# A two-layer encoder trunk on one core: layer 0's output banks emptied by ScalarE and gated on POOL, and a new layout of layer 1's last stage

## The chip, the cores and the metric

The kernel runs on one core of one Trainium2 chip. TensorE (PE) multiplies matrices, VectorE (DVE), ScalarE (ACT) and GpSimd (POOL) do the rest on rows of 128 partitions, and SyncE (SP) issues nearly all DMA transfers. The metric is the device time of one execution in microseconds. Each engine works through its own list of instructions in the order in which the program gives them, and waits at an instruction whose inputs or buffers aren't there yet.

## The reference, cut to what matters

2048 tokens of width 1024 go through two layers. Each layer modulates its input, mixes it, and adds the gated result to the residual ahead of a LayerNorm:

```python
h = x * (1.0 + scale) + shift                    # per layer, shift/scale/gate from c
y = even_mixer(h) if layer == 0 else odd_mixer(h)
x = layer_norm(DEEPNORM_ALPHA * x + gate * y, ln_g[layer], ln_b[layer])

# even_mixer: windowed attention and chunked spatial gating side by side, times silu(g), then
return y @ w_out                                 # (2048, 1024) @ (1024, 1024): the out-projection

# odd_mixer: in-projection, depthwise conv, two gated linear recurrences, then
y = rg_lru(forward) + rg_lru(reverse)            # h[s] = a[s] * h[s-1] + b[s], and the same from the end
return (y * silu(g)) @ w_out
```

The change touches the end of layer 0 (`gate * y` and the residual after the out-projection) and the end of layer 1 (the reverse recurrence's completion and its out-projection). Everything is float32.

## The kernel before, in words

**Matmuls.** The tokens are worked in four tiles `t` of 512. A float32 product is made of three matmuls (`mm3`, L158, L159, L160) on operands split in a high and a low half: the high half is a copy on ACT (L154), the low half a subtraction on DVE (L155). So each operand of a matmul costs one ACT and one DVE instruction, unless it was split earlier and parked in DRAM (`w_d`, `wo_d`).

**Layer 0's out-projection** (`project_out`) runs once per tile `t`. For each half `n` of the output columns, `job_tm` loads eight weight tiles (`raw`), splits each (`hl`) and accumulates into four PSUM banks, one for each 128 tokens. Six banks (`pja`, `px`, `pjb`, two each) go round, so that the next job takes over the banks of an earlier one. When the job is done, DVE multiplies each bank by the gate (`gz`, L753), which frees the bank, and adds ALPHA times the residual (`z`, L755). This makes 4 x 2 x 4 = 32 pairs of instructions. `sgate` is the stage ahead of it; its scratch tile `sq` (L693) stands in the same SBUF pool.

**Layer 1** sweeps forward over `t` = 0..3. Its forward recurrence is finished on the way; the reverse one needs the later tokens, so for t = 0..2 its inputs go to DRAM (`a_d`, `b_d`, `f_d`, `g_d`, `u_d`, `v_d`) and only t = 3 is finished at once: the reverse scan (L1007), the sum of both directions on POOL (L1017), the product with the gate (L1034), and the split into y3[0..7]. The out-projection of t = 3 (`part_out`) keeps its 8 banks over the whole end of the sweep, all PSUM that `pj` and `pm` have: k = 0..3 are added as soon as y3[0..3] are there, k = 4..7 at the end. The out weights wo[n][k] are loaded once and stay in SBUF for all four tiles (`resident`, L1079).

**The way back.** `load_y(t)` makes y for t = 2, 1, 0 from DRAM: for even k a reverse scan (L1113) from the carry of tile t+1, the carry to tile t and the sum with the forward part on POOL (L1116, L1117), and the gate product (L1118); for odd k one multiply-add with the carry (L1127) — both then split. Its tiles `at`, `bt`, `ft`, `gt`, `ut`, `vt` have two buffers each and are loaded on SP (L1106). Then come the out-projection of that tile, the residual rows (`z`, L1151; L1166 for t = 3, L1178 and L1195 for t = 2 and the rest) and the LayerNorm (`norm_rows`: L614, L616, L623, L624), with two POOL instructions for the reciprocal root (L150, L151).

**What sets the order.** The instructions are given in program order to a scheduler that simulates the engines and writes a fixed list for each; `high_priority` moves a piece ahead in it. Nothing is reordered on the chip. SBUF is a stack from each side: the left pool `oq` ("outq") opens where layer 1's front pool (`X`, `xc` and the like) has closed, the right pool `op` ("outp") where the recurrence's pool `rp` (`ra`, `T`, `ii`, `G`, `hg`) has closed. A tile that is laid over an old one waits until the old one's last reader is done, tile by tile.

Of the kernel before, what the change touches and what calls it, by code (L numbers as in the profile page):

```python
# [7 lines left out]
F32 = mybir.dt.float32  # L8
F32R = mybir.dt.float32r
I32 = mybir.dt.int32  # L10
AF = mybir.ActivationFunctionType
ALU = mybir.AluOpType
# [6 lines left out]
KD = D // 128  # L19
C = 512  # L20
NT = S // C
# [32 lines left out]
def kernel(  # L54
# [27 lines left out]
    nc = tc.nc  # L82
    act = nc.scalar.activation
    tt = nc.vector.tensor_tensor
# [154 lines left out]
    for i in range(2):  # L239
        nc.gpsimd.dma_start(out=vrow0[24 + 8 * i:32 + 8 * i].rearrange("k (a q) -> k a q", a=4),  # L240
                            in_=ada_b[1, i * D:i * D + D].rearrange("(a k q) -> k a q", a=4, q=32))
# [4 lines left out]
    ps = bank(px, "px")  # L246
# [22 lines left out]
    ps = bank(px, "px")  # L269
# [26 lines left out]
    ps = bank(px, "px")  # L296
# [331 lines left out]
    bp = pool(sd, "sgate", right)  # L628
    g_bc = bp.tile([128, D], F32, name="g_bc")
    b_bc = bp.tile([128, D], F32, name="b_bc")  # L630
    gate0 = bp.tile([128, D], F32, name="gate0")
# [6 lines left out]
    for g in range(2):  # L638
        wr = bp.tile([128, 4, 128], F32, tag="wsr", bufs=1, name="wsr")
        load(out=wr, in_=ev_sg_w[0, 4 * g:4 * g + 4].rearrange("g p q -> p g q"))  # L640
        ps = bank(pm, "pm")
# [6 lines left out]
    ps = bank(pm, "pm")  # L648
# [3 lines left out]
    for i in range(4):  # L652
        stt(out=bias_sg[:, i, :], in0=ps[:, i * 128:i * 128 + 128], scalar=vcol0[:, 52 + i:53 + i],
            in1=bias_sg[:, i, :], op0=ALU.mult, op1=ALU.add)
# [20 lines left out]
    def sgate(t, hT):  # L675
        cs = cols(w0, 1280)
        if t == 0:
            ps = sv_ps
            count[0] += KD
        else:  # L680
            ps = job_tm(lambda k: wunit(cs(k)), hT)
        sv = []
        for b in range(4):
            pv = ps[b].rearrange("p (g d) -> p g d", g=8)
            mu = bp.tile([128, 8], F32, tag="mu", bufs=2, name="mu")
            with tc.high_priority():
                nc.vector.tensor_reduce(out=mu, in_=pv, axis=AX.X, op=ALU.add)
                ts(out=mu, in0=mu, scalar1=-1.0 / 64.0, scalar2=None, op0=ALU.mult)
            v = bp.tile([128, 8, 64], F32, tag="sv", bufs=5, name="sv")
            sv.append(v)  # L690
            with tc.high_priority():
                tt(out=v, in0=pv, in1=mu[:, :, None].to_broadcast([128, 8, 64]), op=ALU.add)
            sq = bp.tile([128, 8, 64], F32, tag="sq", bufs=2, name="sq")  # L693
            act(out=sq, in_=v, func=AF.Square)
            var = bp.tile([128, 8], F32, tag="var", bufs=2, name="var")
            nc.vector.tensor_reduce(out=var, in_=sq, axis=AX.X, op=ALU.add)
            rsqrt_eps(var, var, 1.0 / 64.0)
            tt(out=v, in0=v, in1=var[:, :, None].to_broadcast([128, 8, 64]), op=ALU.mult)
# [4 lines left out]
        ps = job_cm(lambda k: ug0[k] if k < n0 else wunit(cg(k)), hT)  # L703
# [4 lines left out]
        ps = job_cm(lambda k: wunit(cu(k)), hT)  # L708
# [4 lines left out]
        for i in range(4):  # L713
            ps = bank(pm, "pm")
            for b in range(4):
# [5 lines left out]
                in1=bias_sg[:, i:i + 1, :].to_broadcast([128, 4, 128]), op0=ALU.mult, op1=ALU.add)  # L721
# [6 lines left out]
        ps = job_cm(lambda k: wunit(ca(k), perm=True), hT)  # L728
# [12 lines left out]
    def project_out(t, y):  # L741
        zt = []
        for b in range(4):
            z = bp.tile([128, D], F32, tag="z", bufs=5, name="z")
            load(out=z, in_=xs[t * C + b * 128:t * C + b * 128 + 128, :])
            zt.append(z)
        for n in range(2):
            cw = out_rows(w1, n * C)
            ps = job_tm(lambda k: wunit(cw(k)), y, (4, 5, 6, 7, 0, 1, 2, 3))
            for b in range(4):  # L750
                gz = bp.tile([128, C], F32, tag="gz", bufs=2, name="gz")
                with tc.high_priority():
                    tt(out=gz, in0=ps[b], in1=gate0[:, n * C:n * C + C], op=ALU.mult)  # L753
                zs = zt[b][:, n * C:n * C + C]
                stt(out=zs, in0=zs, scalar=ALPHA, in1=gz, op0=ALU.mult, op1=ALU.add)  # L755
        for b in range(4):
            r = t * C + b * 128
            norm_rows(bp, zt[b], x1_d[r:r + 128, :], g_bc, b_bc)
# [311 lines left out]
    def part_out(ps, hl, k):  # L1070
        for b in range(4):
            sl = slice(b * 128, b * 128 + 128)
            mm3(ps[b], y3[0][k][:, sl], y3[1][k][:, sl], hl[:, 0], hl[:, 1], k == 0, k == KD - 1)

    wo = [[None] * KD, [None] * KD]

    def resident(p, n, k):
        w = p.tile([128, 2, C], F32R, name=f"wo{n}_{k}")
        nc.sync.dma_start(out=w.bitcast(F32), in_=wo_d[n * KD + k])  # L1079
        wo[n][k] = w  # L1080
# [5 lines left out]
            part_out(ps3[n], wo[n][k], k)  # L1086

    oq = pool(ctx, "outq", left)
    for k in (4, 5):
        for n in range(2):  # L1090
            resident(oq, n, k)
    back(NT - 1, 1, f1, G1)
# [6 lines left out]
    def load_y(t):  # L1099
        y = ([], [])  # L1100
        n = C if t < NT - 2 else C - 2
        c0 = t * C

        def fetch(tag, src, k):
            p = oq.tile([128, C], F32, tag=tag, bufs=2, name=tag)
            load(out=p[:, 0:n], in_=src[:, k, c0:c0 + n])  # L1106
            return p

# [24 lines left out]
            y[1].append(lo[:, k % 2])  # L1133
        return y

    y2 = load_y(NT - 2)
    se.close()


    op = pool(ctx, "outp", right)  # L1140
    for k in (6, 7):
        for n in range(2):
            resident(op, n, k)
    for k in range(4, KD):
        for n in range(2):
            part_out(ps3[n], wo[n][k], k)

    def residual_tile(t, b):
        r = t * C + b * 128
# [4 lines left out]
    zt = [residual_tile(NT - 1, b) for b in range(4)]  # L1154
    g_bc = op.tile([128, D], F32, name="g_bc1")
    b_bc = op.tile([128, D], F32, name="b_bc1")
    load(out=g_bc, in_=ln_g[1:2, :].broadcast_to([128, D]))
    load(out=b_bc, in_=ln_b[1:2, :].broadcast_to([128, D]))
    def finish(t, b, z):
# [67 lines left out]
```

## Time and profile before

| | |
|---|---|
| runs of before | 1568.82, 1569.88, 1575.3 us; median 1569.88 us |
| the profiled execution | 1567.64 us, with a span of 1565.9 us from first to last instruction |
| mean granted TensorE clock in it | 0.983 |
| setup and attention, 0 to 440 us of the span | PE busy 410.3 of 440 us |
| layer 0's gating and out-projection, 440 to 905 | PE busy 451.4 of 465 us, DVE 351.1, ACT 160.3, POOL 68.3 |
| layer 1's sweep, 905 to 1395 | PE busy 473.7 of 490 us, DVE 384.4, ACT 351.5, POOL 196.2 |
| between y3[5] and y3[6], 1395 to 1413 | PE busy 0.2 of 18 us, DVE 15.4, ACT 4.9, POOL 8.2 |
| the way back, 1413 to 1566 | PE busy 144.7 of 153 us, DVE 120.0, ACT 11.4, POOL 41.9 |

A row of a timeline gives the start, the time taken, the engine, the line and the operation, then the tiles it writes and reads (buffer numbers left out), and in brackets how long the engine sat idle before it and what ended the idle time. "x2" is two instructions in one row. A row of the list of waits gives the sum, the number and the longest of such idle times. A row of windows gives, for a stretch of the span, its length, each engine's busy time, the granted clock (PEclk, 1.00 is full), the DMA engines' busy share and the GB/s moved. Two matmuls overlap in their pipeline, so in a full stream their starts lie closer together than their durations.

### The profile page before, as it was taken

What the parts mean: (1) busy time and instruction counts of PE and PEld (TensorE: products, weight loads), DVE (VectorE), ACT (ScalarE), POOL (GpSimd) and SP (SyncE); (2) the same over time, 40 slices, a digit from 0 to 9 for tenths busy, and PEclk for the clock granted to TensorE, in tenths of its full rate; (3) what the DMA queues carried; (4) which work ended last, traced back from release to release, by engine and by line L of the source; (5) the groups of instructions that cost most, each with busy time, mean ns of one, the idle gap of its engine ahead of it and who ended that gap; (6) DMA issues with size and microseconds to landing.
All of it is one profiled execution on the core that took longest, in us unless ns stands there. A gap on an engine that the chain in (4) does not pass through costs nothing. (4 is left out here: it accounts for less than half of the span.)

```text
span 1565.9 us, 22099 instructions
## 1 busy us (share of the span) xinstructions
PE 1480.2 (95%) x7096; PEld 1185.7 (76%) x7096; DVE 1186.2 (76%) x2180; ACT 784.1 (50%) x1470; POOL 404.7 (26%) x488
## 2 busy tenths in 40 slices
PE   7999999989999999999999999999999999869997
PEld 3887777657878777788887787787788788747886
DVE  4599889755859568967767775987987697788985
ACT  4677767542523332343244228499498496841100
POOL 1023233211005000300120231634644432133221
PEclk9999999999999999999999999999999999989999
DMA  9357766839788989988785699788777766369751
GB/s 348 130 170 219 224 196 189 265 120 304 243 281 298 257 255 298 314 276 262 260 296 177 195 263 275 231 259 283 224 249 271 236 226 220 111 204 340 257 193 54
DMA packets 209211, 370.91 MB, mean 237 GB/s; under 512 B 56616, under 2 KB 103620, under 8 KB 209096
## 3 DMA queue, kind: packets, MB, share of 16 engines
q1 hardware_dynamic: 202344, 354.53, 70.2%
q0 software_dynamic: 6752, 14.98, 3.7%
q8 instruction: 56, 0.92, 0.2%
q14 instruction: 59, 0.48, 0.1%
HBM read 261.96 MB, written 85.97 MB: 222 GB/s over the span
## 5 line engine op out<-in xcount | busy, mean ns | idle before, releaser
L154 ACT ACTIVATE hl<-raw 128x512 fp32r<-128x512 f32 x192 | 119.1, 628 | 227.3 <-DMA raw<-in_ev_w_in_dram 142.2
L159 PE MATMUL pj<-alo,hl 128*128 128x512 f32 x512 | 200.7, 392 | 0.0
L158 PE MATMUL pj<-ahi,hl 128*128 128x512 f32 x512 | 199.5, 392 | 1.1 <-DVE gz L753 1.1
L160 PE MATMUL pj<-ahi,hl 128*128 128x512 f32 x512 | 199.6, 391 | 0.0
L155 DVE TENSOR_TENSOR hl<-raw,hl 128x512 fp32r<-128x512 f32 x192 | 131.8, 695 | 71.5 <-ACT hl L154 70.7
L150 POOL TENSOR_SCALAR rstd<-mv 128x1 f32<-128x1 f32 x32 | 31.0, 970 | 416.5 <-DVE mv L616 305.8
L158 PEld LDWEIGHTS pj<-ahi,hl 128*128 128x128 f32 x512 | 96.5, 189 | 22.0 <-DVE gz L753 1.5
L159 PEld LDWEIGHTS pj<-alo,hl 128*128 128x128 f32 x512 | 96.6, 189 | 20.3
L160 PEld LDWEIGHTS pj<-ahi,hl 128*128 128x128 f32 x512 | 96.4, 188 | 20.2
L465 POOL DMA_DIRECT2D P<-T x112 | 62.6, 566 | 177.7 <-DVE nm L430 78.0
L158 PE MATMUL pj<-wqh,hhi 128*128 128x256 f32 (+1 forms) x256 | 88.5, 350 | 2.5 <-ACT hhi L154 1.7
L430 DVE CUSTOM_DVE_ANT_0 P<-psc,mask,nsink 128x384 f32<-128x384 f32 (+1 forms) x128 | 73.8, 593 | 22.1 <-PE psc L429 22.0
L154 ACT ACTIVATE phl<-praw 128x512 fp32r<-128x512 f32 x56 | 35.4, 631 | 105.9 <-DMA praw<-in_od_w_in_dram 51.1
L159 PE MATMUL pj<-wql,hhi 128*128 128x256 f32 (+1 forms) x256 | 88.0, 344 | 0.0
L160 PE MATMUL pj<-wqh,hlo 128*128 128x512 f32 (+1 forms) x256 | 85.7, 347 | 1.5 <-DVE hlo L155 1.5
L977 DVE SCALAR_TENSOR_TENSOR ii<-ii,xc 128x1024 f32<-128x1024 f32 (+2 forms) x32 | 40.6, 1269 | 57.6 <-ACT ii L971 57.6
L433 ACT ACTIVATE P<-P,nm 128x384 f32<-128x384 f32 (+1 forms) x128 | 76.4, 601 | 10.3 <-DVE nm L430 10.1
L777 POOL TENSOR_TENSOR alo<-hm,ahi 128x512 fp32r<-128x512 f32 x32 | 48.5, 1524 | 118.5 <-DVE hm L776 99.7
L947 DVE SCALAR_TENSOR_TENSOR xc<-X,vcol,xc 128x512 f32<-128x512 f32 (+2 forms) x96 | 75.2, 818 | 0.3
L158 PE MATMUL pm<-xhi,hg 128*128 128x512 f32 (+3 forms) x160 | 55.6, 361 | 14.1 <-ACT xhi L154 6.5
L155 DVE TENSOR_TENSOR phl<-praw,phl 128x512 fp32r<-128x512 f32 x56 | 39.1, 698 | 35.2 <-ACT phl L154 33.0
L775 ACT ACTIVATE ahi<-hm,shift,scale 128x512 fp32r<-128x512 f32 x32 | 25.2, 812 | 74.1 <-DVE hm L774 66.8
(304 smaller groups left out, 4320.1 us busy)
## 6 DMA issues: line engine op xcount, KB each, us to landing
hl<-w_d SPq DMA_DIRECT2D x128, 512.0 KB, 4.7
raw<-in_ev_w_in_dram SPq DMA_DIRECT2D x128, 256.0 KB, 4.0
w_d<-phl SPq DMA_DIRECT2D x40, 512.0 KB, 4.6
aw<-in_ada_w_dram SPq DMA_DIRECT2D x32, 512.0 KB, 6.9
hg<-w_d SPq DMA_DIRECT2D x32, 512.0 KB, 5.4
P<-T SPq DMA_DIRECT2D x104, 96.0 KB, 4.8
P<-T POOLq DMA_DIRECT2D x104, 96.0 KB, 4.2
aw<-in_ada_w_dram SPq DMA_DIRECT2D x8, 1024.0 KB, 7.7
```

What stands on the lines that cost most here:

```text
L150: nc.gpsimd.tensor_scalar(out=dst, in0=src, scalar1=mul, scalar2=EPS, op0=ALU.mult, op1=ALU.add)
L154: act(out=hi, in_=src, func=AF.Copy)
L155: tt(out=lo, in0=src, in1=hi.bitcast(F32), op=ALU.subtract)
L158: nc.tensor.matmul(ps, lhsT=ahi, rhs=bhi, start=first, stop=False)
L159: nc.tensor.matmul(ps, lhsT=ahi, rhs=blo, start=False, stop=False)
L160: nc.tensor.matmul(ps, lhsT=alo, rhs=bhi, start=False, stop=last)
L430: nc.vector.tensor_tensor_reduce(out=p[:, g, 0:W], in0=ps[:, 0:W], in1=mask[:, m0:m0 + W], scale=-0.125, scalar=nsink[:, h:h + 1], op0=ALU ...
L433: act(out=p[:, g, 0:W], in_=p[:, g, 0:W], func=AF.Exp, scale=-1.0, bias=nm[:, h:h + 1], accum_out=rs[:, h:h + 1])
L465: dma.dma_start(out=pv[32 * r:32 * r + 32, 0:nb, i], in_=T[32 * i:32 * i + 32, 0:nk].rearrange("p (j r) m -> p r j m", r=4)[:, r])
L777: nc.gpsimd.tensor_tensor(out=lo[:, j], in0=h, in1=hi[:, j].bitcast(F32), op=ALU.subtract)
L947: stt(out=xc[:, w], in0=xt[:, j0 + j:j0 + j + W], scalar=vcol1[:, 8 * j + g:8 * j + g + 1], in1=xc[:, w], op0=ALU.mult, op1=ALU.add)
L977: stt(out=ii[i][:, :, w], in0=ii[i][:, :, w], scalar=1.0, in1=xc[:, None, w].to_broadcast([128, 2, W]), op0=ALU.add, op1=ALU.mult)
```

## The change

In layer 0, ACT now copies each bank to `gz` and so frees it; POOL multiplies `gz` by the gate; the residual's addition stays on DVE. `gz` has three buffers in place of two, and `sq` one in place of two, in the same pool. At the end of layer 1, all eight out-weight tiles of k = 4..7 are in `oq` on the left (before, k = 6 and 7 were in `op` on the right, allocated after `load_y(2)`). The tiles of `load_y` move from `oq` to `op`, which opens only once the recurrence's pool has closed. In the program's text `load_y(2)` now comes after t = 3's residual rows and ahead of `part_out` for k = 4..7. Lines after L753 have a number one higher until the deleted lines of the end.

```diff
--- before.py
+++ after.py
@@ -690,7 +690,7 @@
             sv.append(v)
             with tc.high_priority():
                 tt(out=v, in0=pv, in1=mu[:, :, None].to_broadcast([128, 8, 64]), op=ALU.add)
-            sq = bp.tile([128, 8, 64], F32, tag="sq", bufs=2, name="sq")
+            sq = bp.tile([128, 8, 64], F32, tag="sq", bufs=1, name="sq")
             act(out=sq, in_=v, func=AF.Square)
             var = bp.tile([128, 8], F32, tag="var", bufs=2, name="var")
             nc.vector.tensor_reduce(out=var, in_=sq, axis=AX.X, op=ALU.add)
@@ -748,9 +748,10 @@
             cw = out_rows(w1, n * C)
             ps = job_tm(lambda k: wunit(cw(k)), y, (4, 5, 6, 7, 0, 1, 2, 3))
             for b in range(4):
-                gz = bp.tile([128, C], F32, tag="gz", bufs=2, name="gz")
+                gz = bp.tile([128, C], F32, tag="gz", bufs=3, name="gz")
                 with tc.high_priority():
-                    tt(out=gz, in0=ps[b], in1=gate0[:, n * C:n * C + C], op=ALU.mult)
+                    act(out=gz, in_=ps[b], func=AF.Copy)
+                nc.gpsimd.tensor_tensor(out=gz, in0=gz, in1=gate0[:, n * C:n * C + C], op=ALU.mult)
                 zs = zt[b][:, n * C:n * C + C]
                 stt(out=zs, in0=zs, scalar=ALPHA, in1=gz, op0=ALU.mult, op1=ALU.add)
         for b in range(4):
@@ -1086,7 +1087,7 @@
             part_out(ps3[n], wo[n][k], k)
 
     oq = pool(ctx, "outq", left)
-    for k in (4, 5):
+    for k in range(4, KD):
         for n in range(2):
             resident(oq, n, k)
     back(NT - 1, 1, f1, G1)
@@ -1102,7 +1103,7 @@
         c0 = t * C
 
         def fetch(tag, src, k):
-            p = oq.tile([128, C], F32, tag=tag, bufs=2, name=tag)
+            p = op.tile([128, C], F32, tag=tag, bufs=2, name=tag)
             load(out=p[:, 0:n], in_=src[:, k, c0:c0 + n])
             return p
 
@@ -1133,17 +1134,10 @@
             y[1].append(lo[:, k % 2])
         return y
 
-    y2 = load_y(NT - 2)
     se.close()
 
 
     op = pool(ctx, "outp", right)
-    for k in (6, 7):
-        for n in range(2):
-            resident(op, n, k)
-    for k in range(4, KD):
-        for n in range(2):
-            part_out(ps3[n], wo[n][k], k)
 
     def residual_tile(t, b):
         r = t * C + b * 128
@@ -1154,6 +1148,11 @@
     zt = [residual_tile(NT - 1, b) for b in range(4)]
     g_bc = op.tile([128, D], F32, name="g_bc1")
     b_bc = op.tile([128, D], F32, name="b_bc1")
+    y2 = load_y(NT - 2)
+    for k in range(4, KD):
+        for n in range(2):
+            part_out(ps3[n], wo[n][k], k)
+
     load(out=g_bc, in_=ln_g[1:2, :].broadcast_to([128, D]))
     load(out=b_bc, in_=ln_b[1:2, :].broadcast_to([128, D]))
     def finish(t, b, z):
```

The scheduler's lists show it at three places. **SP at the end of layer 1**, where t = 2's inputs and the last out weights are loaded. Before (wo_6 and wo_7 follow some 30 rows further down, between later rows of `load_y`):

```order
L1040 DMA y_d<-T 128x2 x2
L1079 DMA wo_4_13363<-wo_d_84 128x1024
L1079 DMA wo_4_13365<-wo_d_92 128x1024
L1079 DMA wo_5_13367<-wo_d_85 128x1024
L1079 DMA wo_5_13369<-wo_d_93 128x1024
L1106 DMA at<-a_d 128x510
L1106 DMA bt<-b_d 128x510
```

and now:

```order
L1080 DMA wo_5_13401<-wo_d_93 128x1024
L1080 DMA wo_6_13403<-wo_d_86 128x1024
L1080 DMA wo_6_13405<-wo_d_94 128x1024
L1080 DMA wo_7_13407<-wo_d_87 128x1024
L1080 DMA wo_7_13409<-wo_d_95 128x1024
L1041 DMA y_d<-T 128x2 x2
L1145 DMA z<-x_d 128x1024 x4
L1107 DMA at<-a_d 128x510
L1107 DMA bt<-b_d 128x510
L1107 DMA ft<-f_d 128x510
```

All eight weight loads now stand together (wo_4 and wo_5 n = 0 ahead of the first row shown), and t = 3's last `y_d` store and its four residual loads stand ahead of the first load of t = 2's inputs.

**DVE at the same place**, where t = 3's last rows and t = 2's y are made. Before, the last of t = 2's rows (the low halves of y2[6], y2[7]) stand ahead of t = 3's final rows:

```order
L155 TENSOR_TENSOR alo<-ft,ahi 128x512
L155 TENSOR_TENSOR alo<-ut,ahi 128x512
L1127 SCALAR_TENSOR_TENSOR ut<-vt,cr,ut 128x510
L1118 SCALAR_TENSOR_TENSOR ft<-ft,gt 128x510
L155 TENSOR_TENSOR alo<-ut,ahi 128x512
L155 TENSOR_TENSOR alo<-ft,ahi 128x512
L1166 SCALAR_TENSOR_TENSOR z<-z,pj 128x512 x2
L614 BN_STATS st_13625<-z 128x6
L614 BN_STATS st_13636<-z 128x6
L1166 SCALAR_TENSOR_TENSOR z<-z,pj 128x512 x2
```

and now the low half of y3[7] (first row) is followed by t = 3's final rows, mixed with t = 2's:

```order
L155 TENSOR_TENSOR alo<-T,ahi 128x512
L1165 SCALAR_TENSOR_TENSOR z<-z,pj 128x512 x2
L614 BN_STATS st_13657<-z 128x6
L1165 SCALAR_TENSOR_TENSOR z<-z,pj 128x512
L614 BN_STATS st_13668<-z 128x6
L1114 SCALAR_TENSOR_TENSOR bt<-at,carry_b,bt 128x510
L1165 SCALAR_TENSOR_TENSOR z<-z,pj 128x512 x2
L1165 SCALAR_TENSOR_TENSOR z<-z,pm 128x512 x2
L1128 SCALAR_TENSOR_TENSOR ut<-vt,cr,ut 128x510
L1165 SCALAR_TENSOR_TENSOR z<-z,pm 128x512
L614 BN_STATS st_13657<-z 128x6
L1119 SCALAR_TENSOR_TENSOR ft<-ft,gt 128x510
```

The first scan of t = 2 (L1114) now stands behind five instructions of t = 3's final rows, and the two kinds of rows alternate for some 40 rows more.

**ACT at the end of layer 0's last out-projection** (t = 3, first half and second half, then layer 1's first bank copies). Before:

```order
L775 ACTIVATE ahi<-hm,shift,scale 128x512
L154 ACTIVATE phl<-praw 128x512
L154 ACTIVATE hl<-raw 128x512 x4
L154 ACTIVATE phl<-praw 128x512
L775 ACTIVATE ahi<-hm,shift,scale 128x512 x4
L897 ACTIVATE X<-pj 128x512 x4
```

and now:

```order
L776 ACTIVATE ahi<-hm,shift,scale 128x512
L154 ACTIVATE phl<-praw 128x512
L154 ACTIVATE hl<-raw 128x512 x3
L753 ACTIVATE gz<-pjb 128x512 x2
L753 ACTIVATE gz<-pja 128x512
L154 ACTIVATE phl<-praw 128x512
L154 ACTIVATE hl<-raw 128x512
L753 ACTIVATE gz<-pja 128x512
L776 ACTIVATE ahi<-hm,shift,scale 128x512 x4
L753 ACTIVATE gz<-px 128x512 x2
L753 ACTIVATE gz<-pjb 128x512 x2
L898 ACTIVATE X<-pj 128x512 x4
```

Eight bank copies (L753) stand between the splits of the weights (`hl`) and of the parked weights (`phl`); before there was none.

## The prediction, on record before the changed kernel was run

> **What bounds the kernel now.** First the page's busy shares: PE is the bound.
>
> ```profile
> span 1565.9 us, 22099 instructions
> PE 1480.2 (95%) x7096; PEld 1185.7 (76%) x7096; DVE 1186.2 (76%) x2180; ACT 784.1 (50%) x1470; POOL 404.7 (26%) x488
> ```
>
> So a change gains only where PE stands still. I read PE's list of waits next, for lines that the change touches:
>
> ```profile
> PE pj L158 <- DMA wo<-wo_d: 17.9, 1, 17.9
> PE px L158 <- DVE gz L753: 2.3, 1, 2.3
> PE pjb L158 <- DVE gz L753: 2.0, 1, 2.0
> PE pj L158 <- DVE gz L753: 1.1, 1, 1.1
> ```
>
> Four waits: 17.9 us at the end of layer 1, 5.4 us at the bank changes in layer 0. Windows (length, then PE, weight loads, DVE, ACT, POOL busy, then clock, DMA share and GB/s) show that a wait also costs clock:
>
> ```profile
> 440.00:905.00 465.00, 451.40 (x2121) 366.33 (x2120) 351.10 (x587) 160.27 (x270) 68.31 (x61) 0.99 0.82 262
> 455.00:475.00 20.00, 17.72 (x72) 14.12 (x71) 12.93 (x23) 4.44 (x8) 0.00 (x0) 0.91 0.99 347
> 865.00:880.00 15.00, 12.82 (x50) 9.65 (x49) 11.52 (x17) 5.72 (x9) 3.41 (x3) 0.89 0.72 176
> 1413.00:1420.00 7.00, 7.00 (x25) 5.55 (x26) 2.73 (x4) 1.27 (x2) 1.28 (x1) 0.79 1.04 411
> ```
>
> Around the 2.3 us wait the clock is 0.91 over 20 us (1.8 us lost), around the 2.0 us wait 0.89 over 15 us (1.65). I price a wait of 2 us and more at itself plus 1.7.
>
> The large wait, on PE and on SP's queue:
>
> ```profile
> 1394.54 0.39 PE L160 MATMUL pm<-wo,alo 128*128 128x512 f32 x1
> 1412.82 0.77 PE L158 MATMUL pj<-wo,ahi 128*128 128x512 f32 x1 [17.89 <-DMA wo<-wo_d]
> 1425.52 0.39 PE L158 MATMUL pj<-hl,ahi 128*128 128x512 f32 x1
> 1469.42 0.39 PE L158 MATMUL pj<-hl,ahi 128*128 128x512 f32 x1
> ```
>
> ```profile
> 1378.61 2.19 SPq L1079 DMA_DIRECT2D wo<-wo_d  x4
> 1380.85 0.44 SPq L1106 DMA_DIRECT2D at<-a_d  x1
> 1396.08 0.99 SPq L1040 DMA_DIRECT2D y_d<-T  x2
> 1406.06 0.42 SPq L1079 DMA_DIRECT2D wo<-wo_d  x1
> ```
>
> wo[.][6] is issued only at 1406.06, behind the loads of t = 2, and lands at 1412.8. PE then does t = 3's last 48 matmuls (1412.82 to 1425.52, 12.7 us), t = 2's 192 (to 1469.42, 43.9 us, or 0.2287 each) and then t = 1 and t = 0, with the last LayerNorm and store 96.5 us to the span's end at 1565.9. When PE restarts, t = 2's y is nearly made. The wait was filled:
>
> ```profile
> 1391.32 2.06 DVE L1007 TENSOR_TENSOR_SCAN T<-ra,ii 128x514 f32<-128x514 f32 x1
> 1393.35 1.26 DVE L1113 TENSOR_TENSOR_SCAN bt<-at,carry_b,bt 128x510 f32<-128x510 f32 x1
> 1397.80 0.68 DVE L155 TENSOR_TENSOR alo<-T,ahi 128x512 fp32r<-128x512 f32 x1
> 1404.75 0.69 DVE L1118 SCALAR_TENSOR_TENSOR ft<-ft,gt 128x510 f32<-128x510 f32 x1 [1.16 <-POOL ft L1117]
> 1409.11 0.69 DVE L1118 SCALAR_TENSOR_TENSOR ft<-ft,gt 128x510 f32<-128x510 f32 x1 [1.29 <-POOL ft L1117]
> 1413.38 0.75 DVE L1127 SCALAR_TENSOR_TENSOR ut<-vt,cr,ut 128x510 f32<-128x510 f32 x1 [0.55 <-DMA ut<-u_d]
> 1416.82 0.69 DVE L1118 SCALAR_TENSOR_TENSOR ft<-ft,gt 128x510 f32<-128x510 f32 x1 [2.69 <-DMA wo<-wo_d]
> 1418.21 0.69 DVE L155 TENSOR_TENSOR alo<-ft,ahi 128x512 fp32r<-128x512 f32 x1
> ```
>
> From t = 2's first scan (1393.35) to its last low half (1418.9) DVE takes 25.5 us, 5.7 of them waiting (1.16, 1.29, 0.55, 2.69).
>
> **The end of layer 1: what is removed, and what is late next.** All eight weights are now issued together, near 1378, so y3[6] and y3[7] themselves release PE. y3[6]'s low half ended at 1398.5; without t = 2's first scan ahead of it, near 1397.3. The first hi-only products start before that; I let the 48 matmuls start at 1396.7 and take 11.0 (48 x 0.2287): done at 1407.7, where before it was 1425.5. **17.8 us are there to be won.**
>
> They are not won whole, because t = 2's y is late. Its tiles now lie over the recurrence's: the first `at` must wait until y3[7]'s low half is written (1398.4) and T's last store has read it, and behind four residual loads. Issue near 1399; in the chain of waits a fetch took
>
> ```profile
> 1380.85 6.44 DMA at<-a_d
> ```
>
> 6.44 us, so it lands near 1405.4, 18 us later than in before (1387.3). And DVE's fixed list now mixes t = 3's final rows into t = 2's. Their prices, from start to start:
>
> ```profile
> 1422.12 1.28 DVE L614 BATCH_NORM_STATS2 st<-z 128x6 f32<-128x512 f32 x2
> 1423.32 1.27 DVE L1166 SCALAR_TENSOR_TENSOR z<-z,pj 128x512 f32<-128x512 f32 x2
> 1433.10 2.46 DVE L624 SCALAR_TENSOR_TENSOR z<-z,rstd,b_bc 128x1024 f32<-128x1024 f32 x2
> 1435.48 1.27 DVE L1113 TENSOR_TENSOR_SCAN bt<-at,carry_b,bt 128x512 f32<-128x512 f32 x1
> 1436.68 0.25 DVE L616 BATCH_NORM_AGGREGATE mv<-st 128x2 f32<-128x12 f32 x2
> ```
>
> 0.60 for a row of 512, 1.19 for one of 1024, 1.20 for a scan, 0.12 for an aggregate; the odd tiles' multiply-add I take at 0.66. In the new list, from t = 3's first final row up to the gate product of y2[4], stand 8 additions of z, 8 statistics, 4 low halves and 3 gate products (23 x 0.60 = 13.8), 4 first and 2 second passes of the norm (6 x 1.19 = 7.1), 4 scans (4.8), 3 multiply-adds (2.0) and 4 aggregates (0.5): 28.2 us. The first can start when bank 0 of n = 0 is done, 27 matmuls after 1396.7: 1402.9. Waits inside: t = 2's scans, POOL sums and transfers are the ones that made 5.7 us above. t = 3's rows would now cover some of them, and the new round trips (two buffers a tile, released one round later) would add some; bounds are 0 and about 14 (the rival below). I take 5.7, the only measured value. With 0.7 for the rest of the product and ACT's high half, y2[4] reaches PE at 1402.9 + 28.2 + 5.7 + 0.7 = 1437.5.
>
> By PE's new list 84 of t = 2's 192 matmuls stand ahead of y2[4]. The first y2 is ready near 1412.7 (scan behind three additions and two statistics: 1405.9 to 1407.1, POOL to 1409.6, its product in the list at 1411.4, ACT to 1412.7), so these 84 x 0.2287 = 19.2 us fit into 1412.7 to 1437.5. From there 108 x 0.2287 = 24.7 us remain: t = 1 starts at 1462.2 instead of 1469.4. The 96.5 us behind it are as before. **Tail: -7.2 us.** Bounds: no wait in DVE's list leaves PE the limit, 1412.7 + 43.9 = 1456.6, -12.8; 14 us of waits give +1.1.
>
> The other moves here cost nothing that shows: the `fetch` rows and the residual loads are the same transfers in another order, and g_bc and b_bc are needed only by the norm, late in the list.
>
> **Layer 0.** Prices: the DVE product, a bank copy on ACT by layer 1's (same shape, same source), a POOL product by the nearest 128x512 row.
>
> ```profile
> L753 DVE TENSOR_TENSOR gz<-pjb,gate x16: 669/682/684, 443.8 to 898.7; 128x512 f32<-128x512 f32 x16
> L897 ACT ACTIVATE X<-pj x32: 578/600/631, 918.2 to 1288.5; 128x512 f32<-128x512 f32 x32
> L777 POOL TENSOR_TENSOR alo<-hm,ahi x32: 1278/1300/2213, 862.3 to 1237.4; 128x512 fp32r<-128x512 f32 x32
> ```
>
> DVE loses 32 x 0.60 = 19 us, ACT gains 32 x 0.60 = 19, POOL 32 x 1.30 = 42 (bounds 1.28 to 2.21 each). All of it lies beside matmuls: in 440 to 905 (first row of the windows) PE is busy 451 us, DVE 351, ACT 160, POOL 68. Without that cover nothing follows but a later residual row, which nobody on PE waits for. What counts is when the bank is free:
>
> ```profile
> 466.84 0.63 ACT L154 ACTIVATE hl<-raw 128x512 fp32r<-128x512 f32 x1 [2.74 <-DMA raw<-in_ev_w_in_dram]
> 469.05 1.27 DVE L753 TENSOR_TENSOR gz<-px,gate 128x512 f32<-128x512 f32 x2
> 875.46 0.68 DVE L753 TENSOR_TENSOR gz<-pjb,gate 128x512 f32<-128x512 f32 x1
> 876.49 0.63 ACT L154 ACTIVATE hl<-raw 128x512 fp32r<-128x512 f32 x1 [1.67 <-DMA raw<-in_ev_w_out_dram]
> ```
>
> At 469 DVE's product was behind `modulation`'s rows while ACT was idle: that wait goes, -2.3 - 1.7 = -4.0. At 875 ACT is the busier: its copies now stand behind the split that waits for `raw` until 876.49, so the bank comes at about 877.1 + 0.6 instead of 875.46 + 0.68: +1.6. A like order at 613 may cost 1.0 (0 to 2). At 898 nothing changes. **Layer 0: -1.4 us**, bounds -8.8 (all three waits with two clock losses gone) and about +4. The third `gz` buffer and the lost `sq` buffer delay no bank.
>
> A rule of the Trainium skill speaks against this part: "SBUF — State Buffer", section "SBUF: two separate sides", says that DVE with two SBUF inputs and a GpSimd operation that reads SBUF share one port pair as an exclusive lock, so that one blocks the other for a whole instruction. The trace agrees: the scan at 1391.32 took 2.06 beside a POOL sum, against 1.20 at 1435.48. By the rule POOL's 42 us could hold DVE for longer than the 19 it is given back; DVE would then stand at 351 - 19 + 42 = 374 of 465 us and the sum stays.
>
> **Total**: -7.2 - 1.4 = -8.6, so the profiled execution goes from 1567.64 to 1559.0 and the median, which lies 2.2 above it, from 1569.88 to **1561.3**.
>
> **The rivals.**
> *B, y2 is not late.* DVE's waits vanish under t = 3's rows and the gap at 875 doesn't grow: -12.8 - 4.0, up to -12.8 - 8.8: 1553.1 down to 1548.3. For it: both POOL waits in the list above (2.5 us) are short enough for two rows to cover. Against: 18 us later inputs.
> *C, the wait only moves.* t = 2's list waits 14 us instead of 5.7, since each fetch is now needed soon after it is issued: two rounds, each late by most of a 6.44 us fetch, give 5.7 + 2 x 4.2. The tail gives +1.1, with layer 0 the median is 1569.6; 1564 to 1574 between. For it: in 1413 to 1420 the DMA engines are full (share 1.04, 411 GB/s). Against: 84 matmuls and 28 us of DVE rows stand in between.
> *D, slower: ACT's queue.* ACT empties banks in order with splits that wait for weights:
>
> ```profile
> ACT hl L154 <- DMA raw<-in_ev_w_in_dram: 142.2, 69, 10.2
> ```
>
> that is 2.06 us on average. Where a copy stands behind such a split, PE loses 2.06 + 1.7 = 3.8 at the bank change. There are eight. With the tail's 7.2 and the 4.0 of 469 won, three struck even it out and five reach +0.5%; with six the median is 1569.9 - 11.2 + 22.8 = 1581.5. For it: the copies stand among splits in ACT's new list. Against: a late weight holds PE anyway, and PE has other banks' work first.
>
> **How the numbers follow.** Forecast 0.47 (1557 to 1566), B 0.17, C 0.26, D 0.10. A measurement of this kernel can't tell less than about 0.5% (7.8 us) from no change: faster means under 1562.0, slower over 1577.7. The forecast sits near that bound and gives 0.33 faster and 0.14 same; B is faster; C is 0.24 same and 0.02 slower; D is 0.02 same and 0.08 slower: 0.50, 0.40, 0.10. The range leaves out half of B and most of D: 1552 to 1572; the forecast's own is 1557 to 1566.
>
> **What would show it.** Right: PE's 17.9 us wait for `wo` gone; t = 3's last matmuls done near 1408; PE waiting a few us for y2[0] (DVE or ACT rows of L155, L154) near 1408 to 1413 and again before y2[4]; t = 1 starting near 1461; no `gz` wait near 468, a longer one near 875. Wrong: t = 2's `at` landing before 1400 or after 1410, t = 1 starting before 1457 or after 1467, or new waits of PE for ACT's copies at several bank changes.

## The result, and the profile after

The changed kernel takes 1584.09 us (median of 5 runs, 1580.84 to 1592.1) against 1570.51 for the kernel before (5 runs): the ratio on record is 1.0072, with a 95% interval of 1.0046 to 1.0099 (the two medians alone give 1.0086). The forecast was 1561.3 us, faster; it is slower. The profiled execution of the changed kernel took 1592.1 us (span 1590.4), the longest of the five and 8 us above the median, so its stages are read for where the time went, and the sizes come from the ratios further down.

The page's busy shares and PE's list of waits of the changed kernel (sum, number, longest):

```profile
span 1590.4 us, 22131 instructions
PE 1494.6 (94%) x7096; PEld 1193.1 (75%) x7096; DVE 1191.4 (75%) x2148; ACT 799.3 (50%) x1502; POOL 454.9 (29%) x520
```

```profile
PE px L158 <- DVE gu L711: 9.2, 5, 3.9
PE pj L158 <- ACT ahi L154: 7.8, 1, 7.8
PE pm L205 <- DVE parts L201: 6.4, 1, 6.4
PE pjb L158 <- ACT gz L753: 3.5, 1, 3.5
PE pj L158 <- ACT gz L753: 1.2, 1, 1.2
```

The 17.9 us wait for `wo` is gone, and a 7.8 us wait for y2[0] (ACT's high half) stands in its place, as forecast in kind (5.0 us from 1407.7 to 1412.7). But DVE, which lost 32 products, is as busy as before (1191.4 against 1186.2), and two waits have grown: `gu` from 1.4 us to 9.2, `parts` from none to 6.4. The change touches neither. A mark that both programs have shows where the time went: the first and the last bank copy of layer 1 (`X`; the row's start times are "first to last"). Before, the row read 918.2 to 1288.5; now:

```profile
L898 ACT ACTIVATE X<-pj x32: 576/598/632, 943.7 to 1322.3; 128x512 f32<-128x512 f32 x32
```

Layer 1 starts 25.5 us later, the last X is 33.8 us later. The last matmul of before, and then, of the changed kernel, the last matmul ahead of the wait for y2[0], the first of t = 2, the first of t = 1 and the last of all:

```profile
1557.28 0.39 PE L160 MATMUL pm<-wo,alo 128*128 128x512 f32 x1
```

```profile
1440.07 0.39 PE L160 MATMUL pm<-wo,alo 128*128 128x512 f32 x1
1448.29 0.80 PE L158 MATMUL pj<-hl,ahi 128*128 128x512 f32 x1 [7.83 <-ACT ahi L154]
1494.38 0.39 PE L158 MATMUL pj<-hl,ahi 128*128 128x512 f32 x1
1581.72 0.39 PE L160 MATMUL pm<-wo,alo 128*128 128x512 f32 x1
```

The last one starts at 1581.72 instead of 1557.28, 24.4 later, where the medians differ by 13.6. From the last X to the last matmul the program takes 259.4 us instead of 268.8: **in this execution the end of layer 1 won 9.4 us, layer 1 started 25.5 later, and the sweep took 8 longer.** The matmul of the spatial gating (L717) that starts at 400.0 us in before starts at 402.7 now, so that 2.6 of the 25.5 were lost ahead of it. The windows from this matmul to the start of layer 1, before and after (length, PE, weight loads, DVE, ACT, POOL busy, clock, DMA share, GB/s):

```profile
400.00:918.00 518.00, 504.40 (x2365) 409.87 (x2362) 385.03 (x636) 176.63 (x299) 74.92 (x70) 0.99 0.82 263
```

```profile
402.60:943.70 541.10, 512.16 (x2368) 413.15 (x2365) 388.51 (x606) 192.80 (x332) 126.09 (x102) 0.97 0.80 252
```

PE stands idle 28.9 us instead of 13.6 (+15.3) and is busy 7.8 us longer for the same matmuls but three, at a clock of 0.97 instead of 0.99. So a third of the 23.1 us that are lost here is slower matmuls. POOL has 51 us more to do, and DVE, without its products, 3.5 us more.

### The profile page after: what moved, and what is told of

Read it like the earlier page. It is cut to its first block, busy times and chain, and to the rows that moved or that the text cites. A ratio compares the mean times of both kernels' runs of the same rounds, so it can differ in the third digit from the quotient of the medians.

```text
span 1590.4 us, 22131 instructions
## 1 busy us (share of the span) xinstructions
PE 1494.6 (94%) x7096; PEld 1193.1 (75%) x7096; DVE 1191.4 (75%) x2148; ACT 799.3 (50%) x1502; POOL 454.9 (29%) x520
## 5 line engine op out<-in xcount | busy, mean ns | idle before, releaser
L754 POOL TENSOR_TENSOR gz<-gz,gate 128x512 f32<-128x512 f32 x32 | 46.7, 1482 | 299.3 <-ACT gz L753 299.2
L430 DVE CUSTOM_DVE_ANT_0 P<-psc,mask,nsink 128x384 f32<-128x384 f32 (+1 forms) x128 | 73.9, 595 | 24.2 <-PE psc L429 24.1
L158 PE MATMUL pm<-xhi,hg 128*128 128x512 f32 (+3 forms) x160 | 56.5, 368 | 17.9 <-ACT xhi L154 6.5
L183 DVE SCALAR_TENSOR_TENSOR macc<-aw,cond,macc 128x512 f32<-128x512 f32 x56 | 42.2, 753 | 29.7 <-DMA aw<-in_ada_w_dram 29.2
```

The lines of the kernel that those rows point to most:

```text
L158: nc.tensor.matmul(ps, lhsT=ahi, rhs=bhi, start=first, stop=False)
L183: stt(out=acc, in0=aw[:, j], scalar=cond[:, k:k + 1], in1=acc, op0=ALU.mult, op1=ALU.add)
L430: nc.vector.tensor_tensor_reduce(out=p[:, g, 0:W], in0=ps[:, 0:W], in1=mask[:, m0:m0 + W], scale=-0.125, scalar=nsink[:, h:h + 1], op0=ALU ...
L754: nc.gpsimd.tensor_tensor(out=gz, in0=gz, in1=gate0[:, n * C:n * C + C], op=ALU.mult)
```

## The experiments

All times are ratios to the kernel before, on the same chips, with 95% intervals. The theory at first was that layer 0 lost everything, and that the new operations and the new place of other instructions in the lists could both be the reason.

**The two halves apart.** Only the end of layer 1 (layer 0 as before):

```diff
     oq = pool(ctx, "outq", left)
-    for k in (4, 5):
+    for k in range(4, KD):
...
-            p = oq.tile([128, C], F32, tag=tag, bufs=2, name=tag)
+            p = op.tile([128, C], F32, tag=tag, bufs=2, name=tag)
```

(`load_y(2)` and `part_out` are moved as in the change.)

> The change's end of layer 1 alone (weights of k = 4..7 on the left, load_y's tiles on the right, residual rows ahead of load_y(2)); layer 0 as before. My theory (T): this part did in the changed kernel what was forecast, some 9 us less than before from the point where the sweep's last job starts to the end; so the median falls by 7 to 11 us (1560 to 1563) and the whole loss of the change is layer 0's. Rival: the end gains only because layer 0 had come late and its loads with it; then it alone gives less than 4 us.

Measured: 0.9946 (0.9924 to 0.9967), 1564.23 us, about 8.5 us less (the median lies 1.2 above the range). Its last X starts at 1289.8 and its last matmul at 1549.37: 259.6 us between, as in the changed kernel. The end's gain does not hang on layer 0.

Only layer 0's part:

```diff
-            sq = bp.tile([128, 8, 64], F32, tag="sq", bufs=2, name="sq")
+            sq = bp.tile([128, 8, 64], F32, tag="sq", bufs=1, name="sq")
...
-                gz = bp.tile([128, C], F32, tag="gz", bufs=2, name="gz")
+                gz = bp.tile([128, C], F32, tag="gz", bufs=3, name="gz")
                 with tc.high_priority():
-                    tt(out=gz, in0=ps[b], in1=gate0[:, n * C:n * C + C], op=ALU.mult)
+                    act(out=gz, in_=ps[b], func=AF.Copy)
+                nc.gpsimd.tensor_tensor(out=gz, in0=gz, in1=gate0[:, n * C:n * C + C], op=ALU.mult)
```

> Layer 0's part alone (copy on ACT, product on POOL, gz three buffers, sq one); the end of layer 1 as before. T: 18 to 28 us slower than before (1588 to 1598), nearly all of it between 440 and 1000 us of the span, so that this part and the end's part together give the changed kernel. Rival (the parts act on each other): about the changed kernel's 1584, no more than 14 us slower.

Measured: 1.0149 (1.0119 to 1.018), 1597.06 us, some 24 us more. The halves add up: 1.0149 - 0.0054 = 1.0095, inside the change's own interval.

**Layer 0 in parts.** Only the buffer counts, the product on DVE:

```diff
-            sq = bp.tile([128, 8, 64], F32, tag="sq", bufs=2, name="sq")
+            sq = bp.tile([128, 8, 64], F32, tag="sq", bufs=1, name="sq")
...
-                gz = bp.tile([128, C], F32, tag="gz", bufs=2, name="gz")
+                gz = bp.tile([128, C], F32, tag="gz", bufs=3, name="gz")
```

> Only the two buffer counts (sq one, gz three); the product stays on DVE as before. If the single sq buffer is what holds layer 0 (ACT's square waits until DVE has summed the last one, and the banks of that job come late): most of the loss, 12 us or more slower than before. If the operations' new engines or the new order of the lists do it: within 4 us of before.

Measured: 1.0026 (1.0002 to 1.005), 4 us. The single `sq` buffer isn't the cause of most of the loss. And the copy on ACT with the product, from SBUF, on DVE:

```diff
+                    act(out=gz, in_=ps[b], func=AF.Copy)
-                nc.gpsimd.tensor_tensor(out=gz, in0=gz, in1=gate0[:, n * C:n * C + C], op=ALU.mult)
+                tt(out=gz, in0=gz, in1=gate0[:, n * C:n * C + C], op=ALU.mult)
```

> Layer 0's part with the copy on ACT, but the product from SBUF on DVE instead of POOL (buffers as in the change). If POOL is the cause (its products of 1.3 to 2.6 us hold DVE's instructions, and DVE's residual rows wait for them): within 6 us of before. If ACT's copies in its list, or the order of the lists around them, are the cause: 15 us or more slower than before.

Measured: 1.0078 (1.0043 to 1.0112), 12 us, between the two theories. Without POOL half of the loss stays. But the scheduler also writes other lists for each of these kernels: without counting the `gz` rows, about 100 places of DVE's list differ from before in the run with the buffers alone, 135 with layer 0's part, 151 here. To compare operations, the lists had to be held.

**Operations and lists apart.** In the next runs every instruction but the `gz` rows is chained, engine by engine, in a given order (dependencies that order the issue and wait for nothing):

```diff
+    for name, runs in ORDER.items():
+        seq = [lists[name][k] for a, m in zip(runs[::2], runs[1::2]) for k in range(a, a + m)]
+        for p, q in zip(seq, seq[1:]):
+            tc.add_manual_dep(q, p.name, mybir.DependencyInfo(mybir.DependencyClass.NoSync,
+                                                              mybir.DependencyReason.DATA), reason="given order")
```

`ORDER` is the list of the kernel before, or that of layer 0's part alone. First the change's operations in the list of before, then the operations of before in the new list, then copy on ACT and product on DVE in the list of before:

> Layer 0's part with the change's operations and buffers (copy on ACT, product on POOL), but every other instruction of every engine held to the list of before (order-only dependencies; the copies and products stand where the scheduler puts them between). Theory O (the lists: the cheaper gate product let the scheduler draw other rows, splits of weights to be parked whose loads come late, ahead of rows that free a bank): 8 us or less slower than before. Theory P (the operations: POOL's products hold DVE's two-input instructions for some 20 us, and DVE's residual rows wait for POOL): 16 us or more slower, as layer 0's part alone was (24).

> The converse: the gate product on DVE as before (buffers as in the change), every other instruction held to the list of layer 0's part alone. Theory O: 16 us or more slower than before. Theory P: within 8 us of before.

> Copy on ACT and product from SBUF on DVE, everything else held to the list of before. It prices ACT's copy alone, without POOL and without a new order. Theory P: within 5 us of before (the bank waits for ACT's splits in place of DVE's rows). If ACT's queue is what costs (rival D of the prediction): 10 us or more slower, with PE waiting for ACT's copies at three or more bank changes.

Measured, with the start of layer 1 from the rows below as a check (all with the change's buffers):

| gate product | list of before | new list |
|---|---|---|
| on DVE, from PSUM | 1.0026 (scheduler's own list, buffers alone) | 1.0082 (1.0053 to 1.0111) |
| copy on ACT, product on DVE | 1.0028 (1.0005 to 1.0051) | not run (scheduler's own list: 1.0078) |
| copy on ACT, product on POOL | 1.0109 (1.0087 to 1.013) | 1.0149 (1.0119 to 1.018) |

In this order: buffers alone, ACT and DVE in the old list, the old operations in the new list, the change's operations in the old list, layer 0's part:

```profile
L897 ACT ACTIVATE X<-pj x32: 578/602/633, 920.4 to 1294.7; 128x512 f32<-128x512 f32 x32
```

```profile
L898 ACT ACTIVATE X<-pj x32: 576/599/630, 918.6 to 1292.9; 128x512 f32<-128x512 f32 x32
```

```profile
L897 ACT ACTIVATE X<-pj x32: 577/598/629, 932.0 to 1304.9; 128x512 f32<-128x512 f32 x32
```

```profile
L898 ACT ACTIVATE X<-pj x32: 572/599/629, 934.8 to 1311.6; 128x512 f32<-128x512 f32 x32
```

```profile
L898 ACT ACTIVATE X<-pj x32: 577/600/630, 942.4 to 1316.8; 128x512 f32<-128x512 f32 x32
```

Against 918.2 before: +2.2, +0.4, +13.8, +16.6, +24.2. ACT's copy costs nothing that shows by itself, and holding the list costs nothing that shows either. By these starts POOL's product costs 16 us where the lists are the same (934.8 - 918.6), and the new list 12 where the operations are the same (932.0 - 920.4). Each start is that of one execution: in the four runs of the end alone and of its variants, where the rows of layer 0 and of the sweep stand as in before, layer 1 starts at 919.8 to 922.6. The times, of 4 to 10 executions each, give less: **POOL's product costs about 13 us (1.0109 against 1.0028), the new list about 9 (1.0082 against 1.0026), and both together 19 (1.0149 against 1.0026).** Of the two theories neither is enough alone: the change's operations in the old list (17 us over before) lie in theory P's range, the old operations in the new list (13 us) in neither's.

*What POOL does.* The first products in the changed kernel, POOL's row and DVE's:

```profile
449.55 5.96 POOL L754 TENSOR_TENSOR gz<-gz,gate 128x512 f32<-128x512 f32 x4 [81.84 <-ACT gz L753]
```

```profile
450.89 1.75 DVE L756 SCALAR_TENSOR_TENSOR z<-z,gz 128x512 f32<-128x512 f32 x1 [1.18 <-POOL gz L754]
452.68 0.69 DVE L614 BATCH_NORM_STATS2 st<-z 128x6 f32<-128x512 f32 x1
453.39 0.96 DVE L155 TENSOR_TENSOR hl<-raw,hl 128x512 fp32r<-128x512 f32 x1
454.27 1.78 DVE L756 SCALAR_TENSOR_TENSOR z<-z,gz 128x512 f32<-128x512 f32 x1
```

POOL is at its four products from 449.55 to 455.51; all 32 take 1.27 to 1.76 us each, not up to 2.6 as expected above. DVE's addition, which reads two SBUF tiles, takes 1.75 and 1.78 us beside them; the statistics, which read one, take 0.69 as always. The groups (count, busy, mean ns, idle before), before and then after:

```profile
L755 DVE SCALAR_TENSOR_TENSOR z<-z,gz 128x512 f32<-128x512 f32 x32 | 21.0, 675 | 0.0
L614 DVE BATCH_NORM_STATS2 st<-z 128x6 f32<-128x512 f32 x64 | 42.3, 680 | 0.3
L201 DVE COPY parts<-macc 128x256 f32<-128x256 f32 x8 | 2.0, 285 | 0.0
```

```profile
L756 DVE SCALAR_TENSOR_TENSOR z<-z,gz 128x512 f32<-128x512 f32 x32 | 33.3, 1044 | 9.6 <-POOL gz L754 9.6
L614 DVE BATCH_NORM_STATS2 st<-z 128x6 f32<-128x512 f32 x64 | 42.8, 682 | 0.3
L201 DVE COPY parts<-macc 128x256 f32<-128x256 f32 x8 | 4.2, 554 | 0.0
```

The additions alone take 12.3 us more (33.3 - 21.0) and wait 9.6 for POOL. Summed over all of DVE's instructions that overlap a `gz` product on POOL, each against the median of its line without overlap, DVE loses 20 us: what it was to gain. In one place this meets PE's path, since the instruction held is one that PE waits for. The two copies before, and POOL's row and theirs now:

```profile
613.18 0.49 DVE L201 COPY parts<-macc 128x256 f32<-128x256 f32 x2
```

```profile
628.00 2.65 POOL L754 TENSOR_TENSOR gz<-gz,gate 128x512 f32<-128x512 f32 x2 [17.99 <-ACT gz L753]
628.17 2.62 DVE L201 COPY parts<-macc 128x256 f32<-128x256 f32 x2
```

Two copies that took 0.49 us before now end with POOL's second product, 2.1 us later than they would. That is a third of PE's 6.4 us wait; until 624.16 DVE had stood 4.0 us for the split of a weight to be parked, and no `gz` product ran from 610 to 628 us:

```profile
624.16 0.69 DVE L155 TENSOR_TENSOR phl<-praw,phl 128x512 fp32r<-128x512 f32 x1 [4.00 <-ACT phl L154]
```

In the run with the change's operations in the old list the copies took 0.50 us, but the two additions ahead of them, which read two SBUF tiles and took 1.53 before, were held for 1.9 us:

```profile
621.87 3.17 POOL L754 TENSOR_TENSOR gz<-gz,gate 128x512 f32<-128x512 f32 x2 [16.86 <-ACT gz L753]
622.17 3.42 DVE L183 SCALAR_TENSOR_TENSOR macc<-aw,cond,macc 128x512 f32<-128x512 f32 x2
```

PE's wait for `parts` was 5.6 us there, 0 before and 0.3 with the product on DVE in the same list:

```profile
PE pm L205 <- DVE parts L201: 5.6, 1, 5.6
PE px L158 <- DVE gu L711: 4.7, 3, 3.0
```

With POOL at work, about 9 of the 15 us that this run is behind the one with the product on DVE (both from the matmul near 400 us on) are lost at this one matmul, in the wait and in slower matmuls behind it; 4.6 more are lost at a `gu` wait near 840 us, where no `gz` product runs (see below). That POOL's product costs this time is shown by the two runs; how 1.9 us of held additions become a wait of 5.6 is not.

The Trainium skill's "SBUF — State Buffer", section "SBUF: two separate sides", has the rule for this: one port pair is shared by GpSimd and those DVE operations that have two SBUF inputs or run in a mode that uses both ports, and whoever comes first keeps it for the whole instruction. The trace agrees in both directions, 1.75 us for two inputs and 0.69 for one. The two copies read one SBUF tile and were held as well (2.62 us); of the rule's two cases this would be the mode, which no row of the trace shows.

*What the new list does.* In the run of the old operations in the new list, PE waits for `gu`, the product that empties the banks of the spatial gate's input:

```profile
PE px L158 <- DVE gu L711: 7.9, 3, 5.5
```

It was 1.4 us before:

```profile
PE px L158 <- DVE gu L711: 1.4, 3, 0.8
```

The longest, 5.5 us, at t = 3, on SP and on DVE:

```profile
828.26 0.47 SPq L787 DMA_DIRECT2D praw<-in_od_w_out_dram  x1
```

```profile
832.43 0.69 DVE L788 TENSOR_TENSOR praw<-praw,gate 128x512 f32<-128x512 f32 x1 [4.08 <-DMA praw<-in_od_w_out_dram]
833.87 0.69 DVE L155 TENSOR_TENSOR phl<-praw,phl 128x512 fp32r<-128x512 f32 x1 [0.74 <-ACT phl L154]
834.48 0.68 DVE L711 TENSOR_TENSOR gu<-px,gu 128x512 f32<-128x512 f32 x1
```

DVE stands 4.08 us at a weight that is only to be parked for layer 1, and `gu` stands behind it. In before the same three rows follow each other, and DVE stands nearly as long:

```profile
818.24 0.75 SPq L787 DMA_DIRECT2D praw<-in_od_w_out_dram  x1
822.45 0.69 DVE L788 TENSOR_TENSOR praw<-praw,gate 128x512 f32<-128x512 f32 x1 [3.85 <-DMA praw<-in_od_w_out_dram]
```

But there PE waits only 0.3 us for that `gu`: relative to PE's work the load was issued some 5 us earlier. The place isn't the new list's alone: with POOL's products in the old list PE waits 3.0 us at the same `gu`, behind the same load. At t = 1 the new list has a parked split between the two `gu` rows, and three weight splits instead of two ahead of them. Nor are the `gu` waits the whole: from the matmul near 400 us to the start of layer 1 PE stands idle 21.7 us in this run and 16.6 with the buffers alone, and its matmuls take 9.6 us more. Two more runs asked which list does it; the edit is in `ORDER`, in short (the second is the converse):

```diff
-ORDER: the new list for all five engines
+ORDER: the new list for SP, the list of before for PE, DVE, ACT and POOL
```

> Gate product on DVE as before (buffers of the change). SP's list is that of layer 0's part alone, the lists of the other four engines are those of before. The new order everywhere was 1.0082 of before, the buffers alone 1.0026. Theory SP (loads for weights to be parked are issued at other places, come late, and hold the splits that stand ahead of bank-freeing rows): most of the new order's cost is here, 1.006 or more. Theory DVE (the places of the rows in DVE's and ACT's lists do it): 1.004 or less.

> The converse: SP's list of before, the lists of PE, DVE, ACT and POOL of layer 0's part alone, the gate product on DVE. Theory SP: 1.004 or less. Theory DVE: 1.006 or more, with PE waiting 5 us or more for gu products.

Measured: 1.0105 (1.0075 to 1.0135) with only SP's list new, 1.0136 (1.0101 to 1.0171) with only the others new. Both are over 1.006, so neither theory came out: no single list carries the cost. Neither mixture is faster than the whole new list (1.0082); whether they are slower, the intervals don't tell. That the order of the loads and the order of their users were made for each other would explain it, but isn't shown. Which rows of the new list cost how much stays open beyond the `gu` waits.

**Half the dose of POOL** (banks 1 and 3, list of before):

```diff
-                nc.gpsimd.tensor_tensor(out=gz, in0=gz, in1=gate0[:, n * C:n * C + C], op=ALU.mult)
+                (nc.gpsimd.tensor_tensor if b % 2 else tt)(out=gz, in0=gz, in1=gate0[:, n * C:n * C + C], op=ALU.mult)
```

> Copy on ACT, every other instruction held to the list of before, and the product on POOL for banks 1 and 3 only, on DVE for 0 and 2: half the dose of POOL. None was 1.0028 of before, all 32 were 1.0109. If POOL's products cost by their number (each holds DVE for its length): about 1.007, 4 to 9 us above none. If it is one or two places where a POOL product lies beside a row that PE needs: below 1.005 or as much as all.

Measured: 1.0089 (1.0066 to 1.0111). It lies three quarters of the way from none to all, and its interval holds half the way as well as all: inconclusive (9.6 us above none, where 4 to 9 was expected of a cost by number). PE waits at the same matmuls as with the full dose (3.6 us for `parts`; 2.8 for `gu` near 830, 3.0 there with the full dose), which speaks for places rather than number, but doesn't settle it.

**The end of layer 1: why only half of its 17.8 us was won.** In the run with the end alone PE waits 7.95 us for y2[0], and the chain of waits runs over a residual load (first row); when DVE had nothing left ahead of t = 2's first scan, that scan still waited 1.47 us for its inputs:

```profile
1399.28 8.18 DMA z<-x_d
1408.90 1.28 DVE L1113 TENSOR_TENSOR_SCAN bt<-at,carry_b,bt 128x510 f32<-128x510 f32 x1 [1.47 <-DMA gt<-g_d]
1415.72 0.79 PE L158 MATMUL pj<-hl,ahi 128*128 128x512 f32 x1 [7.95 <-ACT ahi L154]
```

Three variants. `at` and `bt` on the left, so that the scans can run early:

```diff
-            p = op.tile([128, C], F32, tag=tag, bufs=2, name=tag)
+            p = (oq if tag in ("at", "bt") else op).tile([128, C], F32, tag=tag, bufs=2, name=tag)
```

> The end of layer 1 as in the change, layer 0 as before, but the tiles at and bt of load_y stay in the left pool, so that t = 2's first scans can run before y3[7] is written; ft, gt, ut and vt stay on the right. In the run with the end alone PE waited 7.95 us for y2[0]. My theory (y2[0] is late because its inputs wait for the recurrence's tiles): the wait falls to 2 to 5 us, and the time to 3 to 6 us under that run's 1564. Rival (DVE's list with t = 3's rows holds it): the wait stays at 7 or more and the time at 1562 to 1566.

Measured: 0.9964 (0.9945 to 0.9983), with a wait of 7.7 us: my theory fell (the median, 1566.61 us, is also 2.4 above that of the end alone); the wait is the one the rival gave, but not for its reason alone. A third `at` now stood in SP's queue ahead of the residual loads and waited for its buffer, so that these were issued at 1409.49, 11.6 us later than in the run with the end alone (1397.86), though the sweep was only 8.4 us later (its last X at 1298.2 against 1289.8):

```profile
1409.12 0.32 SPq L1106 DMA_DIRECT2D at<-a_d  x1
1409.49 2.07 SPq L1144 DMA_DIRECT2D z<-x_d  x4
```

Two of the four residual tiles on the left, and then `load_y(2)` ahead of the other two as well:

```diff
-        z = op.tile([128, D], F32, tag="z", bufs=6, name="z")
+        z = (oq if t == NT - 1 and b < 2 else op).tile([128, D], F32, tag="z", bufs=2 if t == NT - 1 and b < 2 else 5, name="z")
...
+    y2 = load_y(NT - 2)
     zt = [residual_tile(NT - 1, b) for b in range(4)]
     g_bc = op.tile([128, D], F32, name="g_bc1")
     b_bc = op.tile([128, D], F32, name="b_bc1")
-    y2 = load_y(NT - 2)
```

(The second hunk is in the second of these runs only.)

> The end of layer 1 as in the change, layer 0 as before; two of t = 3's four residual tiles lie in the left pool and are loaded before the recurrence's tiles come free. In the run with the end alone four residual loads (2 MB) stood ahead of t = 2's first inputs, landed 7.5 to 9 us after their issue, and made DVE and SP late. Theory: with 1 MB less ahead, t = 2's first scan starts some 2 to 3 us earlier and PE's wait falls from 7.95 to about 5; time 2 to 4 us under the end alone. Rival (t = 2's inputs wait for the recurrence's last reader and the transfers behind it are full anyway): wait 7 or more, time within 2 us of the end alone.

> As the run with two early residual tiles, and load_y(2) ahead of the other two residual tiles in the text, so that t = 2's first twelve loads come before them. Theory: first scan about 5 us earlier than in the end alone, PE's wait for y2[0] 2 to 4 us, time 4 to 7 us under the end alone. Rival (DVE's list: the third and fourth bank's rows of t = 3 now wait for their late residual tiles and hold what stands behind): wait 6 or more, time not under the end alone.

Measured: 0.9928 (0.9911 to 0.9944) with a wait of 5.8 us, and 0.9908 (0.9888 to 0.9928), 1557.52 us, with two short waits instead of one long:

```profile
1412.09 0.50 PE L158 MATMUL pm<-hl,ahi 128*128 128x512 f32 x1 [1.03 <-DVE z L1164]
1413.55 0.73 PE L160 MATMUL pj<-hl,alo 128*128 128x512 f32 x2 [0.72 <-DVE alo L155]
```

With the shift of the last X taken off, the first scan starts 1.9 us earlier than in the end alone in the first of these runs and 5.3 in the second: both as the theory had it. From the last X to the last matmul the second takes 254.0 us (1291.0 to 1544.96), 14.8 under before. So it was the order of the loads that kept y2[0] late. This version, with layer 0 untouched, is the fastest of all: 0.9% under the kernel before, where the changed kernel is 0.7% over it.

## Why the prediction was wrong

**The end of layer 1 (-7.2 forecast): right, about -9.** With the shift of the last X taken off (1.3 us in the run with the end alone), t = 3's matmuls were done at 1406.5 (forecast 1407.7), y2[0] reached PE at 1414.4 (1412.7) and t = 1 started at 1460.7 (1462.2). Two terms inside were off and compensated: the first scan started at 1407.6, not 1405.9, because residual loads of 2 MB went ahead (the runs that moved them brought it forward); and the 5.7 us of waits in DVE's list before y2[4] hardly came, so that the second wait of PE which I forecast near 1437 isn't there. From y2[0] on PE needed 46.3 us for t = 2, 2.4 over its 43.9.

**Layer 0 (-1.4 forecast, bounds -8.8 and +4): wrong by 25 us, and by its bounds.** Three steps failed.

- "By the rule POOL's 42 us could hold DVE for longer than the 19 it is given back; DVE would then stand at 351 - 19 + 42 = 374 of 465 us and the sum stays." The mechanism was named and the rows were in hand (2.06 us against 1.20), but its price was read from an average over the stage. A held instruction costs where it stands: two copies of 0.49 us became 2.62 ahead of a matmul, and POOL's product costs 13 us where all other rows are held in place. It should have been a rival with a price, bounded above by POOL's own 42 us.
- "Without that cover nothing follows but a later residual row, which nobody on PE waits for." DVE's later rows wait behind that row. Of the 9.6 us that DVE waits for POOL, 3.5 stand at three places (450.9, 476.4 and 751.0 us) ahead of splits; the other 6.1 stand at 922.4, ahead of layer 0's last residual rows. How much of the 3.5 reached PE isn't shown.
- "What counts is when the bank is free." I looked at the lists only at the bank changes. Layer 0's part moved other rows at 135 places of DVE's list, and the new lists alone cost some 9 us. The range had no term for it.

The bank changes went as forecast in kind: the wait near 468 (now 474) shrank to 0.74 us, the one near 875 (now 897) grew from 2.0 to 3.5 (forecast +1.6). **Rival D**, the slower one, had the right side and the wrong cause: ACT's copy in the list of before costs nothing that can be told from the buffers alone (1.0028 against 1.0026), and PE's waits for `gz` come to 5.4 us in the changed kernel as in before. Its price per wait, 2.06 us and 1.7 of clock, was high: 15.3 us of idle time came with 7.8 of slower matmuls.

**The sweep** between layer 0 and the end took 378.6 us from the first X to the last, 8.3 more than before, though its rows stand in nearly the same order. Most of this need not be the change's: in the four runs of the end and its variants the sweep stands in the very lists of before, and took 369.1, 371.2, 373.3 and 376.8 us. PE's wait for the weights `hg` was 2.2 us in before, 6.2 in the changed kernel and 4.8 in the run of 376.8, and PE was busy 359.8, 364.5 and 364.2 us. It was 374.3 us with the buffers alone, 374.4 with layer 0's part and 376.8 with the change's operations in the old list. What sets it from one execution to the next stays open.

## What to carry to other kernels

In this kernel, work moved from DVE to POOL was not taken off DVE: price each POOL instruction that reads SBUF as time that DVE's instructions beside it may lose (those with two SBUF inputs, and here two copies), and look which of these a matmul waits for. Compare the whole list of each engine, not only the places that the diff names: in a program that a scheduler orders, a change of one stage's cost moves loads and their users elsewhere too, and the new lists of this case cost as much (about 9 us) as the end of layer 1 won (8.5). Where a wait for one transfer is removed, order the transfers that come next by who needs them first: here this brought 5.6 us on top of 9.2 from the last X to the last matmul.

## What the runs showed of the hardware beyond that

DVE's statistics (one SBUF input) took at most 696 ns, also the nine that overlap a `gz` product on POOL (687 on the mean); DVE's additions of two SBUF tiles took up to 1785 ns instead of 693 at most. In SP's queue a load that waited for its buffer held the loads behind it: the four residual loads of the variant with early scans were issued one after the other from 1409.49, right after the `at` at 1409.12 had got its buffer.
